# The first two pairs of the first feed-forward in two parts by feature chunks, with their loads and steps in another order

## The chip, the cores and the metric

One core of one Trainium2 chip. The metric is the time of one execution in microseconds on the device: 1695.61 us, the median of three runs (1691.41 to 1696.17).

## The reference

One layer of a decoder: a feed-forward (SwiGLU), a token mixer, a second feed-forward, each behind an RMS norm and a shift and scale that are made from a conditioning vector. What matters here is the start:

```
m = silu(c) @ w_ada + b_ada                     # 9 vectors: sh1, sc1, g1, sh2, ...
h = rms_norm(x, n1_g) * (1 + sc1) + sh1
x = x + 0.5 * g1 * (silu(h @ w1_gate) * (h @ w1_up)) @ w1_down
```

x has 512 prompt tokens and 64 sample tokens of 1024 features; the conditioning vector is one for the prompt and one for each of 8 samples. All is float32.

## The kernel before, in words

The tokens stand in the free dimension, 576 of them, in two halves of 288; the 1024 features are 8 chunks of 128 partitions. A float32 product is made of three products of rounded parts: weights and values are each split into a high part (ScalarE, a copy in the rounded type) and a low part (VectorE, the source minus the high part), and `prod` issues high x high, high x low and low x high. A column block of 128 of w1_gate together with the same block of w1_up is a pair. Pairs 0 and 1 are made by `Plain` in four product steps each, with 4 feature chunks per step: h0a (weights n11 and n21, from the first 512 rows, by the operand N11), h1a (the same weights by N1), h0b (weights a12 and a22, from rows 512 to 1023, by B21) and h1b (the same by B22). Each step is 24 products of 128x288, 12 into each of two PSUM banks. Pair 2 and those after it are made by `Pair`, in seven steps of 12, of which P1 (a11 by N11) is the first. The products of pairs 0 and 1 are 192.

The operands need the modulation. The class `First` loads the columns of sh1 and sc1 out of w_ada in four parts of 256 features each: part p covers chunks 2p and 2p+1, in 8 loads of 128x512. For each part there are these steps: mm (8 matmuls by the conditioning vectors, TensorE, L283), M (a copy out of PSUM, ScalarE, L289), tr (4 transposes, TensorE, L295), m (a sum over groups, the bias and the gain a1: three VectorE operations, L300, L304, L363). Then the chunks are normed and modulated: xr (x by the row of reciprocal norms, VectorE, L509), b0 and b1 (scale and bias of the prompt's tokens, ScalarE, L516), s (the same for the sample tokens, VectorE, L525). Operand N11 is minus the first half of chunks 0 to 3, N1 the difference of the halves there (tx is that difference), B21 and B22 are the halves of chunks 4 to 7. The number in N11h0 or B21l3 is the part, h and l are the high and low split. So N11 and N1 need parts 0 and 1, B21 and B22 parts 2 and 3. The sums T2, N3 and N4 are made in place behind them for pair 2. rw is a product with ones on TensorE (L1046) that spreads the reciprocal norms to all partitions, and rr its copy out of PSUM (L1051, L1052); every xr waits for rr.

The order is written out by hand in the table `BEGIN`: `run` executes the steps in its order and adds dependencies, so that on each engine the instructions stand in this order, whatever is ready earlier. The steps nh and nl are the splits of the first half of a pair's weights, wh and wl of the second; sn copies the result of the first half of a pair out of PSUM; xt and xc bring x into place; p2... are the splits and sums of pair 2's weights; e... are the gating, G... the split of a finished pair.

The loads go through one queue of SyncE in the order of the code from L999 to L1007: x, then parts 0 and 1, pair 0 (both halves), part 2, pair 1 (both halves), part 3, pair 2. The raw weights share four buffers (`raw4`), so that pair 2's loads wait for the low splits of earlier ones. B21 and B22 take the buffers of part 2, N3 and N4 those of part 3, so N3h and N4h wait for mm3.

Of the kernel before, what the change touches and what calls it, by code (L numbers as in the profile page):

```python
# [38 lines left out]
BEGIN = """
xt0 xt1 xc0 xt2 xc1 xt3 xc2 xt4 xc3 s5 xt5 xc4 r5 r50 r51 r52 xt6 dg xc5 xt7 xc6 rw xS xc7  # L40
rr xr0 xr3 mm0 xr2 M0 tr0 xr1 mm1 m0 nh0 s0 M1 nl0 b00 tr1 b01 m1 wh0 tx0 b10 s1 b11 wl0
N11h0 N11h1 N11l0 N1h0 N11l1 mm2 tx1 N1l0 N1h1 h0a0 T2a1 M2 N1l1 nh1 T2a0 wh1 nl1 tr2 sn0
h1a0 m2 wl1 b20 b21 s2 B21h2 T2b0 B22h2 h0a1 B21l2 T2h0 N3c0 N4c0 N3h0 T2l0 N4h0 N3l0 mm3
B22l2 sn1 N4l0 M3 tr3 h1a1 m3 b30 s3 b31 B21h3 N3c1 p2ah B21l3 T2b1 h0b1 B22h3 p2al p2bh
T2h1 N3h1 N4c1 B22l3 N4h1 p2S h0b0 T2l1 p2U p2bl p2Sh N3l1 h1b0 p2V N4l1 p2Sl e0s0 e0s1 e0m0
e0m1 h1b1 e1a0 p2Uh e1t0 e1s0 p2Ul e1m0 Gh0 P1 e1a1 e1t1 e1s1 Gl0 P2 e1m1 P1s Gh1 Gl1 P5 P6
P5s P6s
"""
# [31 lines left out]
def layer_kernel(ctx: ExitStack, tc: tile.TileContext, a):  # L80
# [390 lines left out]
    def cost(kc):  # L471
        return kc * 3 * 0.1225
# [124 lines left out]
                else:  # L597
                    st[f"b{p}{c}0"] = lambda p=p, c=c: O.b(2 * p + c, HALF[0])

    def pair_steps(p, greg):  # L600
# [20 lines left out]
        return st

    def prod(ps, w, x, fresh):
        (wh, wl), (xh, xl) = w, x
        for j in range(4):
            for z, (s, m) in enumerate(((wh, xh), (wh, xl), (wl, xh))):
                PE.matmul(  # L627
                    ps[:, :H], lhsT=s[:, j * P:(j + 1) * P], rhs=m[:, j, :],
                    start=fresh and j == 0 and z == 0, stop=j == 3 and z == 2, skip_group_check=True,
                )  # L630
# [45 lines left out]
    class Plain(Weights):  # L676


        def __init__(self, cols, n):
# [1 line left out]
            for z in range(2):
                t = raw4([2, 4, P])
                for i in range(2):
                    self.block_of(t[:, i], i, z)
                self.raw.append(t.rearrange("p m k c -> p m (k c)"))
# [1330 lines left out]
```

## Time and profile before

| | us |
|---|---|
| median of three runs | 1695.61 |
| lowest, highest | 1691.41, 1696.17 |
| the profiled execution: its time | 1692.46 |
| its span (first to last instruction) | 1690.4 |
| TensorE busy in the span | 1650.0 |
| VectorE, ScalarE busy | 1155.7, 784.2 |

The span is what the trace covers; the time of the execution holds 2.06 us more. A step's instructions are found by their lines, and two steps of the same line by their time and their tiles: xa and xs are the buffers of the parts and operands, whl and whs the split weights, wraw the raw weights, hb the normed x, ps a PSUM bank. An engine is the bound of a stretch if it has no idle time there; idle time in front of an instruction is shown with what ended it. TensorE, VectorE, ScalarE, GpSimd and SyncE are PE, DVE, ACT, POOL and SP in the rows, and PEld is the loading of weights into the array.

### The profile page before, as it was taken

The page shows a single profiled execution, that of the slowest core. Times are in us where ns is not written, and L with a number is a line of the kernel's source. Part 1 is how long each engine was busy: PE and PEld are TensorE (multiplying, and loading weights), DVE is VectorE, ACT ScalarE, POOL GpSimd, SP SyncE. Part 2 cuts the span into 40 slices and gives each one's busy share as a digit, 9 for nine tenths or more (in the row PEclk, how much of TensorE's full clock was granted, in tenths as well). Part 3 has the DMA queues.
Part 4 walks back from the last instruction along what each step waited for, and adds up shares of the span by engine and source line. Part 5 has one row for each costly group of instructions (what it writes and reads, how often), then busy time and mean ns, then how long its engine had stood idle before and what let it go on. Part 6 is the DMA issues. An engine that isn't in the chain of part 4 may idle for free.

```text
span 1690.4 us, 31360 instructions
## 1 busy us (share of the span) xinstructions
PE 1650.0 (98%) x12548; PEld 1590.6 (94%) x12548; DVE 1155.7 (68%) x1835; ACT 784.2 (46%) x1331; POOL 288.9 (17%) x372
## 2 busy tenths in 40 slices
PE   7999999999999999999999999998999999999997
PEld 4899999999999998899999999997999999999997
DVE  6867847576797776655697564676748858676773
ACT  5534524344655565544444444443236525343454
POOL 0000000000311111013245442443331000000002
PEclk9999999999999999999999999998999999999999
DMA  9443443342546766664457474898350333232331
GB/s 318 131 146 101 147 140 113 114 123 86 155 146 212 225 187 204 207 209 143 152 181 241 143 176 147 219 250 271 110 180 1 97 91 91 86 99 76 97 92 57
DMA packets 300212, 252.09 MB, mean 149 GB/s; under 512 B 13593, under 2 KB 260633, under 8 KB 300066
## 3 DMA queue, kind: packets, MB, share of 16 engines
q1 hardware_dynamic: 284594, 206.76, 40.3%
q0 software_dynamic: 13168, 40.97, 8.6%
q10 hardware_dynamic: 2304, 2.36, 0.4%
q8 instruction: 98, 1.61, 0.4%
q14 instruction: 48, 0.39, 0.1%
HBM read 207.01 MB, written 43.02 MB: 148 GB/s over the span
## 4 chain that ended last, share of the span: by engine, by line
PE 91%; DVE 3%; DMA 2%; issue 1%; ACT 1%; SPq 1%; POOL 0%; DVEq 0%; POOLq 0%; ACTq 0%
PE ps L627 45%; PE ps L461 30%; PE ps L1325 5%; PE ps L1548 2%; PE ps L283 2%; DMA xa<-in_w_ada_dram 1%; PE ps L1336 1%; PE ps L1415 1%; PE ps L1453 1%; PE ps L1459 1%; PE ps L1431 0%; PE ps L1353 0%; PE ps L295 0%; DMA c<-in_gm_ln_g_dram 0%; DMA xt<-in_x_sample_dram 0%
## 5 line engine op out<-in xcount | busy, mean ns | idle before, releaser
L627 PE MATMUL ps<-xa,whl 128*128 128x288 f32 x3000 | 428.4, 297 | 4.6 <-ACT whl L645 1.4
L627 PEld LDWEIGHTS ps<-xa,whl 128*128 128x128 f32 x3000 | 408.9, 189 | 17.6 <-issue 4.2
L627 PE MATMUL ps<-xs,whl 128*128 128x288 f32 x2040 | 294.1, 297 | 3.4 <-ACT sn L636 3.4
L627 PEld LDWEIGHTS ps<-xs,whl 128*128 128x128 f32 x2040 | 278.5, 189 | 13.5 <-ACT sn L636 6.2
L655 DVE TENSOR_TENSOR whl<-wraw,whl 128x1024 fp32r<-128x1024 f32 x192 | 234.6, 1225 | 58.0 <-ACT whl L645 50.4
L645 ACT CAST whl<-wraw 128x1024 fp32r<-128x1024 f32 x192 | 200.3, 1048 | 104.6 <-DVE wraw L769 61.2
L461 PE MATMUL ps<-c,wd 128*128 128x288 f32 x1824 | 246.1, 295 | 0.0
L461 PEld LDWEIGHTS ps<-c,wd 128*128 128x128 f32 x1824 | 242.9, 188 | 3.4 <-issue 3.4
L461 PE MATMUL ps<-c,whl 128*128 128x288 f32 x1368 | 191.6, 299 | 4.3 <-DVE S L1492 3.2
L461 PEld LDWEIGHTS ps<-c,whl 128*128 128x128 f32 x1368 | 184.6, 189 | 6.3 <-DVE S L1492 3.9
L448 POOL TENSOR_TENSOR x<-x,s 128x64 f32<-128x64 f32 x72 | 34.3, 477 | 814.8 <-DVE s L447 813.2
L442 DVE SCALAR_TENSOR_TENSOR x<-ps,gate,x 128x288 f32<-128x288 f32 (+1 forms) x128 | 61.2, 481 | 118.6 <-PE ps L461 118.5
L165 DVE TENSOR_TENSOR whl<-wraw,whl 128x1024 fp32r<-128x1024 f32 x56 | 77.9, 1393 | 75.8 <-ACT whl L164 73.1
L636 ACT COPY sn<-ps 128x288 f32<-128x288 f32 x195 | 77.4, 398 | 107.3 <-PE ps L627 106.5
L928 ACT CAST wd<-wraw 128x640 fp32r<-128x640 f32 (+2 forms) x58 | 45.3, 781 | 106.9 <-PE ps L461 101.4
L1325 PE MATMUL ps<-whl,xx 128*128 128x256 f32 x768 | 91.6, 279 | 0.0
L1325 PEld LDWEIGHTS ps<-whl,xx 128*128 128x128 f32 x768 | 90.7, 188 | 0.0
L164 ACT CAST whl<-wraw 128x1024 fp32r<-128x1024 f32 x56 | 58.6, 1048 | 31.8 <-PE ps L461 23.2
L627 PE MATMUL ps<-xs,whs 128*128 128x288 f32 x480 | 70.2, 295 | 0.0
L645 ACT CAST whs<-wraw 128x512 fp32r<-128x512 f32 x62 | 38.4, 620 | 66.8 <-PE ps L627 59.2
L627 PEld LDWEIGHTS ps<-xs,whs 128*128 128x128 f32 x480 | 65.7, 188 | 0.0
L933 DVE TENSOR_TENSOR wd<-wraw,wd 128x640 fp32r<-128x640 f32 (+2 forms) x58 | 53.9, 930 | 9.9 <-ACT wd L928 9.8
(285 smaller groups left out, 2226.7 us busy)
## 6 DMA issues: line engine op xcount, KB each, us to landing
ada<-in_w_ada_dram SPq DMA_DIRECT2D x56, 512.0 KB
wraw<-in_w_in_dram SPq DMA_DIRECT2D x96, 256.0 KB
wraw<-in_w_gate_dram SPq DMA_DIRECT2D x88, 256.0 KB
wraw<-in_w_up_dram SPq DMA_DIRECT2D x88, 256.0 KB
...
```

The costliest lines, as they stand in the source:

```text
L164: ACT.copy(out=hi, in_=raw)
L165: (eng or DVE).tensor_tensor(out=lo, in0=raw, in1=hi.bitcast(F32), op=ALU.subtract)
L442: DVE.scalar_tensor_tensor(out=x[:, o:o + w], in0=ps[:, :w], scalar=g[:, c, 0:1], in1=x[:, o:o + w], op0=ALU.mult, op1=ALU.add)
L448: return lambda: POOL.tensor_tensor(out=x[:, NP:T], in0=x[:, NP:T], in1=u, op=ALU.add)
L461: PE.matmul(ps[:, :H], lhsT=s[:, k, c0:c0 + P], rhs=m[:, HALF[h]], start=k == 0 and z == 0, stop=k == kc - 1 and z == 2,)
L627: PE.matmul(ps[:, :H], lhsT=s[:, j * P:(j + 1) * P], rhs=m[:, j, :], start=fresh and j == 0 and z == 0, stop=j == 3 and z == 2, skip_group ...
L636: ACT.copy(out=t, in_=ps[:, :H])
L645: ACT.copy(out=hl[:, 0], in_=src)
L655: DVE.tensor_tensor(out=hl[:, 1], in0=src, in1=hl[:, 0].bitcast(F32), op=ALU.subtract)
L928: ACT.copy(out=hl[:, 0], in_=self.raw[c])
L933: DVE.tensor_tensor(out=lo, in0=self.raw[c], in1=hi.bitcast(F32), op=ALU.subtract)
L1325: PE.matmul(ps[:, :DV], lhsT=s, rhs=m, start=i == 0, stop=i == 23)
```

## The change

The steps h0a, h1a, h0b and h1b of pairs 0 and 1 are cut into two each: h0a and h0c, h1a and h1c, h0b and h0d, h1b and h1d. Each is 12 products, over two feature chunks instead of four, so that a step needs one part of the modulation: a needs part 0, c part 1, b part 2, d part 3. The loads of the first two pairs are cut in halves and stand between the parts: part 0, first half of pair 0, part 1, first half of pair 1, part 2, second half of pair 0, part 3, second half of pair 1, pair 2. And `BEGIN` is written anew from mm0 on.

```
+    def part(self, name):
+        t = "AD"[int(name[1])]
+        z, js = {"a": (0, (0, 1)), "c": (0, (2, 3)), "b": (1, (0, 1)), "d": (1, (2, 3))}[name[2]]
+        if name[2] == "a":
+            setattr(self, t, [bank() for _ in range(2)])
+        x = (("N11", "B21"), ("N1", "B22"))[int(name[1])][z]
+        for ps, w in zip(getattr(self, t), (("n11", "n21"), ("a12", "a22"))[z]):
+            prod(ps, self.w[w], op(x), z == 0, js)
...
-    def prod(ps, w, x, fresh):
+    def prod(ps, w, x, fresh, js=range(4)):
...
-        for j in range(4):
+        for j in js:
...
-    parts = [First(0), First(1)]
...
-    pairs = {0: Plain(cols(w1, 0), 0)}
-    parts.append(First(2))
-    pairs[1] = Plain(cols(w1, 1), 1)
-    parts.append(First(3))
+    pairs, parts = {i: Plain(cols(w1, i), i, ()) for i in range(2)}, []
+    for p in range(4):
+        parts.append(First(p))
+        pairs[p % 2].load(p // 2)
...
-rr xr0 xr3 mm0 xr2 M0 tr0 xr1 mm1 m0 nh0 s0 M1 nl0 b00 tr1 b01 m1 wh0 tx0 b10 s1 b11 wl0
+rr xr0 m0 b00 b01 s0 mm1 M1 N11h0 nh0 N11l0 nl0 tx0 h0a0 xr1 tr1 N1h0 m1 N1l0 b10 b11 s1 nh1 h1a0
```

Three places show what this does to the order of instructions. The first is TensorE right behind the transposes of x: h by ones is rw, xa by cs is mm0, ident by ada is tr0. Before:

```order
L1046 MATMUL ps_294<-h_276,ones 128x128
L1046 MATMUL ps_294<-h_278,ones 128x128
L1046 MATMUL ps_294<-h_280,ones 128x128
L1046 MATMUL ps_294<-h_282,ones 128x128
L1046 MATMUL ps_295<-h_284,ones 128x64
L283 MATMUL ps_312<-xa_150,cs 32x512 x4
L283 MATMUL ps_312<-xa_155,cs 32x512 x4
L295 MATMUL ps_324<-ident,ada_322 128x128 x4
```

and now:

```order
L282 MATMUL ps_294<-xa_150,cs 32x512 x4
L282 MATMUL ps_294<-xa_155,cs 32x512 x4
L1061 MATMUL ps_303<-h_276,ones 128x128
L1061 MATMUL ps_303<-h_278,ones 128x128
L1061 MATMUL ps_303<-h_280,ones 128x128
L1061 MATMUL ps_303<-h_282,ones 128x128
L1061 MATMUL ps_304<-h_284,ones 128x64
L294 MATMUL ps_314<-ident,ada_310 128x128 x4
```

mm0 has moved ahead of rw. The second place is TensorE around the mm steps of parts 2 and 3: xs_28 and xs_29 are part 2, xs_32 and xa_197 (now xs_31 and xa_194) part 3, and a row with whl is one bank of a product step. Before, from mm2 to tr3:

```order
L283 MATMUL ps_377<-xs_28_176,cs 32x512 x4
L283 MATMUL ps_377<-xs_29_181,cs 32x512 x4
L627 MATMUL ps_390<-xa_370,whl_343 128x288 x12
L627 MATMUL ps_391<-xa_370,whl_343 128x288 x12
L295 MATMUL ps_426<-ident,ada_417 128x128 x4
L627 MATMUL ps_435<-xa_374,whl_343 128x288 x12
L627 MATMUL ps_436<-xa_374,whl_343 128x288 x12
L627 MATMUL ps_475<-xa_370,whl_420 128x288 x12
L627 MATMUL ps_476<-xa_370,whl_420 128x288 x12
L283 MATMUL ps_512<-xs_32_192,cs 32x512 x4
L283 MATMUL ps_512<-xa_197,cs 32x512 x4
L295 MATMUL ps_529<-ident,ada_527 128x128 x4
```

and now, from the last of the six steps on N11 and N1 (h0c1) to tr3; xs_84 is B21 and xs_85 is B22:

```order
L630 MATMUL ps_407<-xa_346,whl_385 128x288 x6
L630 MATMUL ps_408<-xa_346,whl_385 128x288 x6
L282 MATMUL ps_469<-xs_28_176,cs 32x512 x4
L282 MATMUL ps_469<-xs_29_181,cs 32x512 x4
L294 MATMUL ps_481<-ident,ada_478 128x128 x4
L630 MATMUL ps_354<-xs_84_497,whl_490 128x288 x6
L630 MATMUL ps_355<-xs_84_497,whl_490 128x288 x6
L630 MATMUL ps_387<-xs_85_501,whl_490 128x288 x6
L630 MATMUL ps_388<-xs_85_501,whl_490 128x288 x6
L282 MATMUL ps_536<-xs_31_189,cs 32x512 x4
L282 MATMUL ps_536<-xa_194,cs 32x512 x4
L294 MATMUL ps_547<-ident,ada_545 128x128 x4
```

mm2 has moved behind six of the half steps (h0a0, h1a0, h0a1, h0c0, h1c0, h0c1), and h0b0 and h1b0 stand between it and mm3. The third place is ScalarE between the copies M of parts 2 and 3 (the rows with ada); hb by mT and a is b, xs and xa are operands' high parts, whl a weight's high part, sn and the h at its side a copy sn. Before, from b of part 2 to M3:

```order
L516 ACTIVATE hb_309<-hb_309,mT,a_149 128x512 x2
L542 CAST xs_81_470<-hb_309 128x576
L542 CAST xs_82_473<-hb_309 128x576
L542 CAST xa_502<-hb_309 128x576
L542 CAST xs_86_506<-hb_309 128x576
L542 CAST xa_509<-hb_309 128x576
L636 COPY sn_522<-ps_475 128x288
L636 COPY h_524<-ps_476 128x288
L289 COPY ada_527<-ps_512 128x512
```

and now, from M2 to wh1:

```order
L288 COPY ada_478<-ps_469 128x512
L648 CAST whl_490<-wraw_186 128x1024
L515 ACTIVATE hb_325<-hb_325,mT,a_149 128x512 x2
L541 CAST xs_84_497<-hb_325 128x576
L541 CAST xs_85_501<-hb_325 128x576
L541 CAST xa_517<-hb_325 128x576
L541 CAST xs_87_521<-hb_325 128x576
L288 COPY ada_545<-ps_536 128x512
L648 CAST whl_556<-wraw_199 128x1024
```

The split of pair 0's second half (whl_490) now stands between M2 and b of part 2, and that of pair 1 (whl_556) behind M3. On VectorE the low parts wl0 and wl1 stand behind the m steps of parts 2 and 3 in the same way. From the first steps of the third pair on, TensorE's rows are those of before.

More of the change, by code (lines that the diff above doesn't have):

```diff
@@ L39 @@
 BEGIN = """
-xt0 xt1 xc0 xt2 xc1 xt3 xc2 xt4 xc3 s5 xt5 xc4 r5 r50 r51 r52 xt6 dg xc5 xt7 xc6 rw xS xc7
-rr xr0 xr3 mm0 xr2 M0 tr0 xr1 mm1 m0 nh0 s0 M1 nl0 b00 tr1 b01 m1 wh0 tx0 b10 s1 b11 wl0
[L42 to L47, printed above, removed]
+xt0 xt1 xc0 xt2 xc1 xt3 xc2 xt4 xc3 s5 xt5 xc4 r5 r50 r51 r52 xt6 dg xc5 xt7 xc6 mm0 rw M0 xS xc7 tr0
+rr xr0 m0 b00 b01 s0 mm1 M1 N11h0 nh0 N11l0 nl0 tx0 h0a0 xr1 tr1 N1h0 m1 N1l0 b10 b11 s1 nh1 h1a0
+N11h1 nl1 tx1 N11l1 N1h1 h0a1 N1l1 h0c0 xr2 sn0 h1c0 T2a0 T2a1 h0c1 sn1 mm2 M2 xr3 tr2 m2 wh0 b20 b21
+s2 wl0 B21h2 B21l2 T2b0 B22h2 B22l2 N3c0 h0b0 T2h0 T2l0 N4c0 N3h0 h1b0 N3l0 mm3 M3 tr3 m3 wh1 b30 b31
+wl1 s3 h0b1 B21h3 B21l3 h1a1 N4h0 N4l0 B22h3 h1c1 N3c1 B22l3 p2ah T2b1 h0d0 p2al T2h1 h1d0 p2bh N3h1 T2l1
+h1b1 N4c1 h0d1 e0s0 p2S N3l1 N4h1 e0s1 p2U e0m0 p2bl p2Sh h1d1 N4l1 e0m1 p2V e1a0 p2Sl p2Uh
+e1t0 e1s0 p2Ul P1 e1m0 Gh0 e1a1 e1t1 e1s1 Gl0 P2 e1m1 P1s Gh1 Gl1 P5 P6 P5s P6s
 """
@@ L598, in norm_steps, with pair_steps @@
                     st[f"b{p}{c}0"] = lambda p=p, c=c: O.b(2 * p + c, HALF[0])
-    def pair_steps(p, greg):
+    def pair_steps(p, greg, parted=False):
         st = {}
@@ L610, in pair_steps @@
         for i in range(2):
+            if parted:
+                for n in ("h0a", "h0c", "h0b", "h0d", "h1a", "h1c", "h1b", "h1d"):
+                    st[f"{n}{i}"] = lambda i=i, n=n: p[i].part(n)
             for n, f in (("nh", "nh"), ("nl", "nl"), ("wh", "wh"), ("wl", "wl"), ("h0a", "h0a"), ("sn", "snaps"),
@@ L613, in pair_steps @@
                          ("e1a", "e1a"), ("e1s", "e1s"), ("e1t", "e1t"), ("e1m", "e1m")):
-                st[f"{n}{i}"] = lambda i=i, f=f: getattr(p[i], f)()
+                st.setdefault(f"{n}{i}", lambda i=i, f=f: getattr(p[i], f)())
             st[f"Gh{i}"] = lambda i=i: G(i, lambda i: p[i].finish_hi())
@@ L630, in prod @@
                 )
-        tick(cost(4))
+        tick(cost(len(js)))
     def snap(ps, t=None):
@@ L676, in layer_kernel, with __init__, load @@
     class Plain(Weights):
-        def __init__(self, cols, n):
+        def __init__(self, cols, n, halves=range(2)):
             self.cols, self.n, self.g, self.w, self.hl, self.raw = cols, n, None, {}, {}, []
[L681 to L685, printed above, removed]
+            for z in halves:
+                self.load(z)
+        def load(self, z):
+            t = raw4([2, 4, P])
+            for i in range(2):
+                self.block_of(t[:, i], i, z)
+            self.raw.append(t.rearrange("p m k c -> p m (k c)"))
+        def part(self, name):
[6 more added lines that the diff above has]
+                prod(ps, self.w[w], op(x), z == 0, js)
         def nh(self):
@@ L1066, in layer_kernel @@
     ops["near"] = ("B21", "B22", "N3")
-    steps = {**operand_steps(Late()), **pair_steps(pairs, greg)}
+    steps = {**operand_steps(Late()), **pair_steps(pairs, greg, True)}
     for c in range(KC):
```

## The prediction

> **What bounds the kernel now.** I read the page first, then the busy times by stretch, then the timeline of each engine up to 70 us. The page says that TensorE is the bound, and the stretches say where:
>
> ```profile
> span 1690.4 us, 31360 instructions
> PE 1650.0 (98%) x12548; PEld 1590.6 (94%) x12548; DVE 1155.7 (68%) x1835; ACT 784.2 (46%) x1331; POOL 288.9 (17%) x372
> ```
>
> In the stretches the columns are length, busy time and count of PE, PEld, DVE, ACT and POOL, then the granted clock, the share of the DMA engines and GB/s:
>
> ```profile
> 0.00:5.00 5.00, 0.68 (x7) 0.71 (x8) 0.00 (x0) 2.34 (x2) 1.40 (x11) 1.00 0.49 140
> 5.00:10.00 5.00, 2.84 (x11) 1.64 (x11) 0.93 (x2) 1.87 (x5) 0.00 (x0) 1.00 1.01 302
> 10.00:15.00 5.00, 5.00 (x20) 3.21 (x19) 2.24 (x5) 4.95 (x17) 0.00 (x0) 1.00 1.09 328
> 15.00:20.00 5.00, 5.00 (x20) 3.66 (x21) 4.12 (x13) 1.33 (x2) 0.00 (x0) 1.00 1.09 384
> 45.00:50.00 5.00, 3.04 (x28) 1.84 (x21) 3.72 (x9) 2.60 (x6) 0.00 (x0) 0.95 0.78 247
> 50.00:55.00 5.00, 5.00 (x29) 5.00 (x29) 4.03 (x7) 4.97 (x8) 0.00 (x0) 0.71 0.36 105
> 48.35:100.00 51.65, 51.65 (x375) 49.54 (x376) 42.19 (x69) 29.29 (x47) 0.00 (x0) 0.97 0.38 113
> 100.00:200.00 100.00, 100.00 (x752) 95.98 (x751) 69.46 (x116) 41.20 (x66) 3.60 (x8) 1.00 0.44 130
> 200.00:400.00 200.00, 199.98 (x1501) 193.59 (x1500) 138.06 (x225) 81.59 (x129) 6.58 (x16) 1.00 0.41 118
> ```
>
> From 48.35 to 400 us TensorE has no gap worth naming (199.98 of 200.00 in the last row). So a change that touches only the first 70 us is worth what it does to one moment: the start of P1, the first product step of the third pair, behind which the two kernels queue the same products. A shift of P1 passes through to the end about one to one.
>
> The PE timeline up to P1 (columns: start, length, engine, line, operation, count, in brackets the idle time before it and what ended it). L1046 is rw, L283 an mm step, L295 a tr step, L627 products:
>
> ```profile
> 18.86 2.69 PE L1046 MATMUL ps<-h,ones 128*128 128x128 f32 x10
> 21.48 3.64 PE L283 MATMUL ps<-xa,cs 128*32 128x512 f32 x16
> 25.90 0.66 PE L295 MATMUL ps<-ident,ada 128*128 128x128 f32 x4 [0.78 <-ACT ada L289]
> 26.49 1.92 PE L283 MATMUL ps<-xa,cs 128*32 128x512 f32 x16
> 29.25 0.66 PE L295 MATMUL ps<-ident,ada 128*128 128x128 f32 x4 [0.84 <-ACT ada L289]
> 32.22 1.69 PE L283 MATMUL ps<-xs,cs 128*32 128x512 f32 x4 [0.26 <-DMA xs<-in_w_ada_dram]
> 33.84 3.87 PE L627 MATMUL ps<-xa,whl 128*128 128x288 f32 x24
> 37.91 6.63 PE L627 MATMUL ps<-xa,whl 128*128 128x288 f32 x48
> 44.47 1.07 PE L283 MATMUL ps<-xs,cs 128*32 128x512 f32 x8
> 45.35 1.04 PE L283 MATMUL ps<-xa,cs 128*32 128x512 f32 x8
> 48.35 0.66 PE L295 MATMUL ps<-ident,ada 128*128 128x128 f32 x4 [1.96 <-ACT ada L289]
> 48.76 4.95 PE L627 MATMUL ps<-xa,whl 128*128 128x288 f32 x24
> 53.55 12.96 PE L627 MATMUL ps<-xs,whl 128*128 128x288 f32 x96
> 66.34 1.76 PE L627 MATMUL ps<-xa,whl 128*128 128x288 f32 x12
> ```
>
> To be seen here: all four mm steps are behind TensorE by 46.4 us, with 72 of the 192 products of pairs 0 and 1 put between them; mm2 ran as soon as its weights came (32.22, a DMA ended the wait). From 48.35 on, 120 products stand back to back until P1 at **66.34**. One product costs 12.79 / 96 = 0.133 us at full clock (53.55 to 66.34). The 24 at 48.76 took 4.79 instead of 3.2, in the stretch whose clock is 0.71: the gap behind mm3 cost **1.6 us** of clock besides its own length.
>
> **The change, part by part.** The work is the same: the 192 products, the four mm and tr steps, the splits, the bytes. Sixteen more rows in PE's order are only groups of 12 cut into 6 and 6. So P1 moves by what PE waits, and that follows from the order. Two effects are free. The loads: the same 14.0 MB (x, c and vec 2.45, four parts of 2.1, three pairs of 1.05, by the tile shapes) come in another order, and nothing below waits for them; part 0 is there when mm0 can start, since 4.55 MB stand ahead of its end in the queue, and the first four rows above bring 0.70, 1.51 and 1.64 by 15 us and the rest by about 17. The buffers of pair 3's second load come free only after wl1 (about 61 us, before: by 44), but its products stand 11 us behind P1. If I am wrong on that cover, it costs the few us of one load.
>
> What costs is the path from the x turns to P1. Its lengths are these rows, of ACT (rowr is rr, L289 is M, L643 is nh, L516 is b, L540 and L542 are the high parts) and of DVE (L509 is xr, four of them; L300 to L363 is m; L651 is nl; L559 is tx; L551 a low part):
>
> ```profile
> 20.97 0.58 ACT L1051 COPY rowr<-ps 128x512 f32<-128x512 f32 x1 [4.62 <-PE ps L1046]
> 25.74 1.06 ACT L643 ACTIVATE whl<-wraw 128x1024 fp32r<-128x1024 f32 x1
> 28.61 0.58 ACT L289 COPY ada<-ps 128x512 f32<-128x512 f32 x1 [1.81 <-PE ps L283]
> 29.09 1.52 ACT L516 ACTIVATE hb<-hb,mT,a 128x512 f32<-128x512 f32 x2
> 32.87 1.24 ACT L540 ACTIVATE xa<-hb 128x576 fp32r<-128x576 f32 x2
> 41.73 1.25 ACT L542 CAST xs<-hb 128x576 fp32r<-128x576 f32 x2
> 21.83 5.17 DVE L509 TENSOR_TENSOR hb<-x,rowr 128x1152 f32<-128x1152 f32 x4 [1.43 <-ACT rowr L1052]
> 26.91 0.30 DVE L300 TENSOR_REDUCE m<-ps 128x36 f32<-128x144 f32 x1
> 27.48 0.18 DVE L363 SCALAR_TENSOR_TENSOR a<-mT,vec 128x18 f32<-128x18 f32 x1
> 28.22 1.22 DVE L651 SCALAR_TENSOR_TENSOR whl<-wraw,whl 128x1024 fp32r<-128x1024 f32 x1
> 29.94 0.31 DVE L300 TENSOR_REDUCE m<-ps 128x36 f32<-128x144 f32 x1 [0.50 <-PE ps L295]
> 30.64 0.76 DVE L559 TENSOR_TENSOR tx<-hb 128x576 f32<-128x576 f32 x1
> 43.02 0.75 DVE L551 TENSOR_TENSOR xs<-hb,xs 128x576 fp32r<-128x576 f32 x1
> ```
>
> An m step is 26.91 to 27.66, so 0.75. From the start of an mm step to the start of its m step, through M and tr, is 26.49 to 29.94: 3.45. A half product step is 12 x 0.133 = 1.6; when it waits for a low part, 10 of its 12 products come after that: 1.35.
>
> *Up to the first half step.* mm0 and rw swap places: together 18.86 to 25.1 as before, but rr, 2.1 behind the start of rw, now waits for mm0 (3.64): it ends at about 25.4 instead of 21.8. Then, in the written order, xr0 (5.17 / 4 = 1.3) 26.7, m0 27.5, b00 and b01 29.0, M1 29.5, N11h0 30.2, nh0 31.2 on ACT, nl0 32.4 on DVE, and the ten products of h0a0 33.8. tr0 and mm1 were done at about 27.5, so PE waits 3.7 us here.
>
> *Up to mm2.* tr1 stands behind h0a0 on PE although M1 was ready at 29.5: tr1 34.5, m1 35.2, b10 and b11 36.8, nh1 37.8, N11h1 38.4; on DVE nl1 39.1, tx1 39.8, N11l1 40.5. So h0c0 ends at 41.9, and h1c0 and h0c1 at **45.1**. Only then comes mm2, whose data landed by about 33, since all six half steps stand ahead of it.
>
> *Up to mm3.* m2 starts 3.45 behind, 48.6, ends 49.4; b20 and b21 51.0, B21h2 51.7, B21l2 52.4, h0b0 53.8, h1b0 55.4. mm3 stands behind these.
>
> *Up to P1.* m3 starts at 58.8 and ends at 59.6; wl1, behind it on DVE, 60.8; h0b1 62.2. h1a1 and h1c1, which need nothing from parts 2 and 3, are queued behind h0b1 and wait with it. From there no operand is late: the seven half steps h1a1, h1c1, h0d0, h1d0, h1b1, h0d1, h1d1 take 11.2. **P1 at 73.4** at full clock, 7.1 later.
>
> As a check from the other side: from the end of mm1 to P1 PE has 192 x 0.133 = 25.5, two mm (3.8) and three tr (1.5), 30.9 us of work, in both kernels. Before, 28.41 to 66.34 leaves 7.0 for waits and the low clock; now 27.5 to 73.4 leaves 15.0.
>
> *The clock.* An mm matmul took 1061 ns at 21.5 us and 592 at 26.5:
>
> ```profile
> L283 PE MATMUL ps<-xa,cs x16: 1059/1061/1062, 21.5 to 24.1; 128*32 128x512 f32 x16
> L283 PE MATMUL ps<-xa,cs x16: 592/592/617, 26.5 to 27.8; 128*32 128x512 f32 x16
> ```
>
> so mm0 at 18.86 is costed at 3.64 (if it ran at 1.92, all is 1.7 earlier). Before, one gap of 1.96 us and a tr cost 1.6 us. Now there are three gaps: 27.5 to 31.2; 47.0 to 51.7 with only a tr in it; 57.3 to about 60.8, with a tr and two products. Behind the first, only 1.35 us of h0a0 stand on the path. Bounds: none costs anything (0), or each costs 1.6 (4.8). I take the two later ones, 3.2, since PE runs on the path right behind them. P1 at 76.6: **10.3 us later**. The Trainium skill (TensorE: Matmul & The Clock Gate, section HAM oscillation) has a rule against this change: gaps of more than about 3.4 us put the array back on half clock, and work behind each starts cold. By it the first two gaps count surely, and the third about evenly; the sum would be 7.1 and 1.35 + 1.6 to 3.2, 10 to 12. The trace is stricter than the rule: a gap of 1.96 us was enough at 49.5.
>
> Sum: the profiled execution took 1692.46 (span 1690.4 and 2.06 around it); 1692.46 + 10.3 = 1702.8. The runs shown had 1691.41, 1695.61 and 1696.17, a median 3.15 above the profiled one, which would give 1705.9. I forecast **1704**.
>
> How this can be read in the order of instructions: in TensorE's rows shown above with the change, no product stands ahead of mm2 in the kernel before, and those between mm2 and mm3 need parts 0 and 1 alone, which are there. Now 72 products stand ahead of mm2, and those between tr2 and mm3 need B21 and B22, the operands that are made out of mm2's own result, through ACT's b and high parts and DVE's low parts. That is why PE runs dry twice, behind mm2 and behind mm3.
>
> **The rivals.** *It does what it says: products fill the waits.* PE would have only its 30.9 us from 27.5 to P1, so P1 at 58.4, 7.9 earlier: 1692.46 - 7.9 = 1684.6. For it: the loads and PE's share allow it. Against it: h0a0 cannot start before nh0, and mm2, h0b0 and mm3 form a chain in which each waits for ACT and DVE work on the part before. It decides on PE's waits from mm1 to P1: under 2.8 us the kernel is faster by over 0.3%, which is 5.1 us and about what a measurement of this kernel can tell from no change. I have 15.0. Chance 0.04.
>
> *The vector work is quicker than its sum.* If mm0 runs at full clock (1.7 earlier) and no gap costs clock, the shift is 7.1 - 1.7 = 5.4; a further 1 us less of waits makes it no difference: 1697 to 1701. Chance 0.14.
>
> *Every gap costs its clock*, and the half clock in h0a0 moves tr1 too: 7.1 + 4.8 = 11.9, and up to 14 if a gap spans two spells of half clock: 1704.4 to 1709. Chance 0.25. The forecast's own case has the rest, 0.57.
>
> **How the numbers follow.** The forecast, the quick case's upper part and most of the third case give 8 in 10: from 1692.46 + 5.0 = 1697.5 to 1695.6 + 13.4 = 1709. Slower by over 0.3%: 0.57 + 0.25 = 0.82; within 0.3%: 0.14; faster: 0.04.
>
> **What would show it.** Right: in the PE timeline of the changed kernel mm2 starts at 43 to 47 and mm3 at 53 to 59, both with data long landed; PE idles about 15 us between mm1 and P1, ended by ACT and DVE; P1 stands at 73 to 79; the granted clock falls below 1 in two or three stretches before 70 us; from P1 on the timeline is that of before, shifted. Wrong: mm2 before 38 us, or h0a0 before 29, or P1 at or before 66; or a shift at P1 that is gone at 400 us.

## The result, and the profile after

The changed kernel took **1704.43 us** (median of 4 runs, 1702.73 to 1705.58) against 1695.38 for the kernel before (4 runs, 1691.41 to 1696.17): a ratio of 1.0063, 95% interval 1.0048 to 1.0078. By the medians it is slower by 9.05 us. The ratio is an estimate over the runs and not the quotient of the two medians (1.0053): by it the difference is 10.7 us, with 8.1 to 13.2 in the interval. Its profiled execution took 1704.38 us.

The page of the profile: TensorE is the bound as before, with the same number of matmuls.

```profile
span 1702.4 us, 31365 instructions
PE 1655.1 (97%) x12548; PEld 1594.8 (94%) x12548; DVE 1154.9 (68%) x1835; ACT 785.6 (46%) x1331; POOL 289.0 (17%) x372
```

PE's timeline of the changed kernel up to P1 (L282 is an mm step, L1061 rw, L294 tr, L630 products):

```profile
18.43 2.64 PE L282 MATMUL ps<-xa,cs 128*32 128x512 f32 x16
21.00 1.52 PE L1061 MATMUL ps<-h,ones 128*128 128x128 f32 x10
...
23.04 3.45 PE L282 MATMUL ps<-xa,cs 128*32 128x512 f32 x16
28.74 0.53 PE L630 MATMUL ps<-xa,whl 128*128 128x288 f32 x2 [2.26 <-ACT whl L646]
30.00 2.64 PE L630 MATMUL ps<-xa,whl 128*128 128x288 f32 x10 [0.72 <-DVE whl L654]
...
44.43 1.92 PE L282 MATMUL ps<-xs,cs 128*32 128x512 f32 x16
47.13 0.66 PE L294 MATMUL ps<-ident,ada 128*128 128x128 f32 x4 [0.79 <-ACT ada L288]
50.89 0.61 PE L630 MATMUL ps<-xs,whl 128*128 128x288 f32 x1 [3.10 <-ACT xs L541]
51.68 5.89 PE L630 MATMUL ps<-xs,whl 128*128 128x288 f32 x23 [0.18 <-DVE xs L550]
57.50 1.06 PE L282 MATMUL ps<-xs,cs 128*32 128x512 f32 x8
...
62.86 1.59 PE L630 MATMUL ps<-xs,whl 128*128 128x288 f32 x10 [1.18 <-DVE whl L658]
...
67.49 8.16 PE L630 MATMUL ps<-xs,whl 128*128 128x288 f32 x60
75.49 1.76 PE L630 MATMUL ps<-xa,whl 128*128 128x288 f32 x12
```

mm2 starts at 44.43 and mm3 at 57.50, where they stood at about 30 and 44.47. Each wait printed in these rows is ended by ScalarE or VectorE, none by a load (one wait for a load hides inside the row of mm1; see old_loads). P1 starts at 75.49, 9.15 us later than before; the medians differ by 9.05. The stretches of the changed kernel (columns as in the prediction: the granted clock is the third number from the end):

```profile
30.00:32.00 2.00, 2.00 (x9) 2.00 (x10) 1.88 (x2) 0.68 (x1) 0.00 (x0) 0.54 1.11 366
32.00:34.00 2.00, 1.73 (x8) 1.41 (x7) 0.43 (x2) 0.00 (x0) 0.00 (x0) 0.60 1.12 370
...
50.00:52.00 2.00, 0.93 (x2) 0.61 (x3) 1.50 (x3) 1.38 (x3) 0.00 (x0) 0.66 0.09 23
52.00:54.00 2.00, 2.00 (x9) 2.00 (x9) 2.00 (x4) 0.67 (x1) 0.00 (x0) 0.50 1.01 272
54.00:56.00 2.00, 2.00 (x10) 2.00 (x10) 0.97 (x2) 0.00 (x0) 0.00 (x0) 0.50 0.66 238
56.00:58.00 2.00, 2.00 (x15) 1.43 (x18) 0.00 (x0) 0.00 (x0) 0.00 (x0) 0.63 0.00 0
...
200.00:400.00 200.00, 199.92 (x1501) 193.58 (x1500) 136.75 (x226) 81.43 (x128) 6.57 (x16) 1.00 0.41 120
```

The clock is at half behind the first pause (30 to 34) and for most of 51 to 57.5 behind the second, where 23 products took 5.89 us instead of 23 x 0.133 = 3.1; behind the third it is full. From P1 on there is nothing new: 199.92 of 200 us are busy.

### The profile page after: what moved, and what is told of

Read it like the earlier page. It is cut to its first block, busy times and chain, and to the rows that moved or that the text cites. A ratio compares the mean times of both kernels' runs of the same rounds, so it can differ in the third digit from the quotient of the medians.

```text
span 1702.4 us, 31365 instructions
## 1 busy us (share of the span) xinstructions
PE 1655.1 (97%) x12548; PEld 1594.8 (94%) x12548; DVE 1154.9 (68%) x1835; ACT 785.6 (46%) x1331; POOL 289.0 (17%) x372
## 4 chain that ended last, share of the span: by engine, by line
PE 85%; issue 5%; DVE 3%; DMA 3%; ACT 2%; POOL 1%; SPq 1%; POOLq 0%; DVEq 0%; ACTq 0%
PE ps L630 40%; PE ps L460 30%; PE ps L1340 5%; PE ps L1563 2%; PE ps L282 1%; PE ps L1351 1%; PE ps L1430 1%; PE ps L1468 1%; DMA xa<-in_w_ada_dram 1%; DMA wraw<-in_w_in_dram 1%; DVE whl L658 1%; PE ps L1474 1%; PE ps L1446 0%; PE ps L1368 0%; PE ps L294 0%
## 5 line engine op out<-in xcount | busy, mean ns | idle before, releaser
L630 PE MATMUL ps<-xa,whl 128*128 128x288 f32 x3000 | 430.3, 298 | 9.6 <-ACT whl L646 2.3
L630 PEld LDWEIGHTS ps<-xa,whl 128*128 128x128 f32 x3000 | 410.1, 190 | 23.4 <-issue 5.0
L630 PE MATMUL ps<-xs,whl 128*128 128x288 f32 x2040 | 297.8, 299 | 7.7 <-ACT xs L541 3.1
L630 PEld LDWEIGHTS ps<-xs,whl 128*128 128x128 f32 x2040 | 281.2, 190 | 18.8 <-ACT sn L639 5.9
L630 PE MATMUL ps<-xs,whs 128*128 128x288 f32 x480 | 70.1, 294 | 0.0
L630 PEld LDWEIGHTS ps<-xs,whs 128*128 128x128 f32 x480 | 65.7, 188 | 0.0
```

What stands on the lines that cost most here:

```text
L630: PE.matmul(ps[:, :H], lhsT=s[:, j * P:(j + 1) * P], rhs=m[:, j, :], start=fresh and j == 0 and z == 0, stop=j == 3 and z == 2, skip_group ...
```

## The experiments

My theory: PE waits longer between mm1 and P1, because mm2 and mm3 stand late and each is followed by its own turn, sums and splits with nothing to do beside them; pauses also let the clock fall; what P1 loses arrives at the end. The main rivals: the loads' order or the cut into half steps costs, or the clock is only a symptom. P1 stood at 66.34, 65.02 and 65.26 us in the three executions that have the order of before (before, half_steps, before_fill), 65.5 on average. Differences in time are of medians, each against the runs of the kernel before that were made beside it.

**old_loads**: only the loads go back to the order of before.

```diff
-    pairs, parts = {i: Plain(cols(w1, i), i, ()) for i in range(2)}, []
-    for p in range(4):
-        parts.append(First(p))
-        pairs[p % 2].load(p // 2)
+    parts = [First(0), First(1)]
+    pairs = {0: Plain(cols(w1, 0), 0)}
+    parts.append(First(2))
+    pairs[1] = Plain(cols(w1, 1), 1)
+    parts.append(First(3))
```

> The order of the steps of the changed kernel, with the order of the loads of the kernel before. Theory (the steps' order makes TensorE wait, the loads land in time either way): the first product step of pair 2 (P1) starts at 75.5 us give or take 1.5, as in the changed kernel, and the ratio to before is 1.0063 give or take 0.001. Rival (the loads' order costs the time): P1 goes back towards the 66.3 us of before, with a ratio of 1.003 or less.

Measured: 1705.30 against 1693.25 us, ratio 1.0075 (1.0061 to 1.0088). PE's timeline:

```profile
18.73 3.64 PE L282 MATMUL ps<-xa,cs 128*32 128x512 f32 x16
...
30.16 0.85 PE L630 MATMUL ps<-xa,whl 128*128 128x288 f32 x2 [3.60 <-ACT whl L646]
...
36.57 9.65 PE L630 MATMUL ps<-xa,whl 128*128 128x288 f32 x59 [1.29 <-DVE xa L550]
...
77.69 1.76 PE L630 MATMUL ps<-xa,whl 128*128 128x288 f32 x12
```

P1 is not earlier but 2.2 us later, beyond my bounds by 0.7, and the waits have the same enders. mm0 took 3.64 us here, against 2.64, so everything hung on rr came later: 1.4 us of the 2.2 stand already at h0a0 (30.16 against 28.74). The rest is the clock, which fell at other places: the 59 products from 36.57 took 9.65 instead of 59 x 0.133 = 7.9, the 23 behind the second pause 4.84 (5.89 in the changed kernel), the ten behind the third 2.48 (1.59) and the 24 behind those 4.02 (3.36). That is TensorE's speed, not a load. The new order of the loads does make mm1 wait: the changed kernel's mm1 took 3.45 us, 1.4 of them waits of its weight loads for part 1, against 1.92 here. But the copy M1 stands on ScalarE behind b0, which ended at 26.50, when that mm1 had just ended (26.49), and so nearly all of it is hidden: M1 follows the start of b0 by 1.60 us there and by 1.42 here. The rival falls.

**half_steps**: the kernel before, each step as two half steps in a row.

```diff
-N11h0 N11h1 N11l0 N1h0 N11l1 mm2 tx1 N1l0 N1h1 h0a0 T2a1 M2 N1l1 nh1 T2a0 wh1 nl1 tr2 sn0
+N11h0 N11h1 N11l0 N1h0 N11l1 mm2 tx1 N1l0 N1h1 h0a0 h0c0 T2a1 M2 N1l1 nh1 T2a0 wh1 nl1 tr2 sn0
```

> The kernel before with the eight steps of the first two pairs cut into half steps that run right behind one another; loads and order as before. Theory (cutting is free, placing costs): P1 at 66.3 us give or take 0.5, ratio 1.000 give or take 0.0007. Rival (the cut itself costs, since TensorE goes 16 times instead of 8 from one bank to the other): 9 us over 8 more changes would be 1.1 us each, and the ratio 1.005.

Measured: 1693.00 against 1693.25 us, ratio 0.9999 (0.9989 to 1.0008). PE's timeline from h0a on, with the 1.95 us pause behind mm3:

```profile
34.45 3.45 PE L631 MATMUL ps<-xa,whl 128*128 128x288 f32 x24
...
48.54 0.66 PE L295 MATMUL ps<-ident,ada 128*128 128x128 f32 x4 [1.95 <-ACT ada L289]
48.95 3.43 PE L631 MATMUL ps<-xa,whl 128*128 128x288 f32 x24
...
65.02 1.76 PE L631 MATMUL ps<-xa,whl 128*128 128x288 f32 x12
```

The cut is free. P1 is 1.3 us earlier than in the profile of before, 0.8 below my bounds, mainly because behind the same pause the 24 products took 3.43 us, not 4.95. (The first 24 took 3.45 instead of 3.87 too, but started 0.6 later, behind mm2's load.) So the 1.6 us that I priced a pause at belonged to one execution and not to the pause.

**earlier23**: the changed kernel with mm2 and mm3 (and what hangs on them) pulled ahead. Pieces of the table:

```diff
-N11h1 nl1 tx1 N11l1 N1h1 h0a1 N1l1 h0c0 xr2 sn0 h1c0 T2a0 T2a1 h0c1 sn1 mm2 M2 xr3 tr2 m2 wh0 b20 b21
+N11h1 nl1 tx1 xr2 N11l1 N1h1 mm2 h0a1 N1l1 M2 tr2 h0c0 sn0 h1c0 m2 T2a0 T2a1 h0c1 sn1 xr3 wh0 b20 b21
-s2 wl0 B21h2 B21l2 T2b0 B22h2 B22l2 N3c0 h0b0 T2h0 T2l0 N4c0 N3h0 h1b0 N3l0 mm3 M3 tr3 m3 wh1 b30 b31
+s2 wl0 B21h2 B21l2 T2b0 B22h2 B22l2 N3c0 mm3 h0b0 M3 tr3 T2h0 m3 T2l0 N4c0 h1b0 N3h0 wh1 b30 b31
```

> The changed kernel with mm2, its copy, turn and sum, and mm3 with its own, moved ahead by one or two half steps, so that products stand between mm2 and tr2, tr2 and h0b0, mm3 and tr3; loads and half steps as in the changed kernel. Theory (what costs is that each part of the modulation stands with its turn and its sum in one row on TensorE with nothing between): two pauses shrink, P1 at 71.5 us give or take 1.5, ratio 1.0038 give or take 0.001. Rival (the later start of the modulation's parts costs little, the half steps or the loads cost): P1 at 74.5 us or later, ratio 1.0055 or more.

Measured: 1699.91 against 1693.25 us, ratio 1.0039 (1.0026 to 1.0052). PE's timeline:

```profile
37.69 1.92 PE L283 MATMUL ps<-xs,cs 128*32 128x512 f32 x16
...
50.17 0.40 PE L631 MATMUL ps<-xs,whl 128*128 128x288 f32 x1 [1.70 <-ACT xs L542]
...
71.19 1.76 PE L631 MATMUL ps<-xa,whl 128*128 128x288 f32 x12
```

mm2 stands 6.7 us earlier, the wait at h0b0 is 1.70 instead of 3.10, P1 is at 71.19. As the theory had it: where the modulation's parts stand is what costs.

**split_first**: nh0 and nl0 of pair 0 ahead of the first modulated blocks.

```diff
-rr xr0 m0 b00 b01 s0 mm1 M1 N11h0 nh0 N11l0 nl0 tx0 h0a0 xr1 tr1 N1h0 m1 N1l0 b10 b11 s1 nh1 h1a0
+rr xr0 m0 nh0 b00 b01 nl0 s0 mm1 M1 N11h0 N11l0 tx0 h0a0 xr1 tr1 N1h0 m1 N1l0 b10 b11 s1 nh1 h1a0
```

> The changed kernel with the split of pair 0's first weights (nh0 on ScalarE, nl0 on VectorE) moved ahead of the first modulated blocks, into time in which ScalarE waits 2.09 us. Theory (the first pause is the queue of ScalarE and VectorE ahead of h0a0, and a wait shortened there passes on): h0a0 starts 0.7 to 1 us earlier and its second wait goes, P1 74.0 us give or take 1.2, ratio 1.0055 give or take 0.0012. Rival (the later links, m1 and what hangs on it, set the end, so nothing comes through): h0a0 earlier, but h0b0 and P1 as in the changed kernel, 75.5 us or later.

Measured: 1701.39 against 1693.59 us, ratio 1.0051 (1.0037 to 1.0066). PE's timeline:

```profile
18.18 3.64 PE L283 MATMUL ps<-xa,cs 128*32 128x512 f32 x16
...
28.52 0.40 PE L631 MATMUL ps<-xa,whl 128*128 128x288 f32 x1 [1.60 <-ACT xa L540]
29.31 1.73 PE L631 MATMUL ps<-xa,whl 128*128 128x288 f32 x11 [0.39 <-DVE xa L547]
...
73.81 1.76 PE L631 MATMUL ps<-xa,whl 128*128 128x288 f32 x12
```

Although mm0 ended 0.75 us later than in the changed kernel (18.18 + 3.64 against 18.43 + 2.64), h0a0's later products start 0.7 earlier, mm2 2.0 (42.42) and P1 1.7 earlier. The first wait is ScalarE's and VectorE's queue, and what is saved there passes on; but that is only the 0.7, and most of what comes on top up to mm2 is the clock, which stayed full behind the first pause (11 products in 1.73 us, against ten in 2.64). Two details were not as expected: h0a0's first product is only 0.2 earlier (28.52), and its second wait is shorter (0.39 instead of 0.72) and not gone.

**after_again**: the changed kernel itself, once more.

> The changed kernel once more, unchanged. Theory (where the clock falls behind a pause, and for how long, differs from one execution to the next of the same instructions): the waits behind the same engines as before within 0.5 us, but P1 not at 75.5 us, somewhere from 74 to 78, with other stretches at half clock. Rival (the clock falls at fixed places): P1 within 0.3 us of 75.49 and half clock in the same stretches. Both: ratio 1.0063 give or take 0.0015.

Measured: 1704.13 against 1693.59 us, ratio 1.0070 (1.0056 to 1.0085). PE's timeline:

```profile
18.25 3.29 PE L282 MATMUL ps<-xa,cs 128*32 128x512 f32 x16
...
51.54 4.85 PE L630 MATMUL ps<-xs,whl 128*128 128x288 f32 x23 [0.40 <-DVE xs L550]
...
61.68 2.51 PE L630 MATMUL ps<-xs,whl 128*128 128x288 f32 x10 [1.18 <-DVE whl L658]
...
75.82 1.76 PE L630 MATMUL ps<-xa,whl 128*128 128x288 f32 x12
```

and two of its stretches:

```profile
62.00:64.00 2.00, 2.00 (x11) 2.00 (x10) 1.39 (x3) 1.97 (x5) 0.00 (x0) 0.50 0.70 236
64.00:66.00 2.00, 2.00 (x12) 2.00 (x12) 2.00 (x4) 0.82 (x1) 0.00 (x0) 0.64 0.54 159
```

P1 is 0.33 us off its first place, hardly beyond the rival's bound, but made up otherwise: the 23 products behind the second pause took 4.85 and not 5.89, and the ten behind the third 2.51 and not 1.59. So the places of half clock differ between two executions of the same instructions.

The stretches also tell how long a spell of half clock lasts, since a stretch of 2 us with a clock of 0.64 was at half for 2 x 2 x 0.36 = 1.44 us, if the clock is either full or half (the undivided stretches read 1.00 or 0.50). Such a spell takes 3.44 us (62.00 to 65.44) in the rows above, and 3.44 (30.16 to 33.60) and 6.84 (50.64 to 57.48) in those of the changed kernel. The other spells before P1 have the same measure: 6.84 (31.28 to 38.12) and 3.44 (51.76 to 55.20) in after_again, 3.44 (49.52 to 52.96) in the profile of before, 10.24 in old_loads. All are one, two or three times 3.4, and between the spells of one execution lie whole multiples of it: 17.04 us from 33.60 to 50.64, 13.64 from 38.12 to 51.76, 6.80 from 55.20 to 62.00. So the clock changes only at points of a fixed grid of 3.4 us within an execution, wherever the pauses lie on it. A spell costs half its length, 1.7 us, where products stand back to back in it, and less where TensorE waits anyway.

**fill_both**: 16 products behind mm1 and 24 behind tr2 that nobody reads. (The second group writes to free columns of the bank in which pair 0's sum stands open, and alters that sum.)

```diff
+        for i in range(16):
+            PE.matmul(ps[:, 0:P], lhsT=ones, rhs=ident, start=True, stop=True, skip_group_check=True)
...
+        for i in range(24):
+            PE.matmul(pairs[0].A[0][:, H:512], lhsT=pairs[1].w["n11"][0][:, 0:P], rhs=op("N1")[0][:, 0, 0:512 - H], start=True, stop=True, skip_group_check=True)
```

> The changed kernel with products that nobody reads in two of TensorE's pauses: 16 of 128x128 behind mm1 and 24 of 128x224 behind tr2. The waits' causes stay as they are. Theory (part of the 9.15 us is half clock behind the pauses, about 1.3 us at h0a0 and 3 us at h0b0 and behind): the granted clock stays full from 23 to 60 us, P1 starts at 71.5 us give or take 1, ratio 1.0035 give or take 0.001. Rival (the waits alone set the time and work beside them is hidden): P1 at 74.5 us or later, ratio 1.0055 or more.

Measured: P1 at 71.60 us, as the theory had it, but 1701.65 against 1693.25 us, ratio 1.0051 (1.0035 to 1.0066), between the two expectations.

**fill_three**: the same in a bank of their own, and a third group behind tr3.

```diff
+    steps["fill1"], steps["fill2"], steps["fill3"] = (lambda n=n, w=w: fill(n, w) for n, w in ((16, 0), (20, 1), (8, 1)))
...
-rr xr0 m0 b00 b01 s0 mm1 M1 N11h0 nh0 N11l0 nl0 tx0 h0a0 xr1 tr1 N1h0 m1 N1l0 b10 b11 s1 nh1 h1a0
+rr xr0 m0 b00 b01 s0 mm1 fill1 M1 N11h0 nh0 N11l0 nl0 tx0 h0a0 xr1 tr1 N1h0 m1 N1l0 b10 b11 s1 nh1 h1a0
```

> The changed kernel with products that nobody reads, into a bank of their own, in three pauses: 16 of 128x128 behind mm1, 20 of 128x288 behind tr2, 8 of 128x288 behind tr3. Theory (the changed kernel loses some 4 us to half clock behind its pauses, in whichever of them it falls): no half clock from 24 to 66 us, P1 at 71.6 us give or take 0.7, ratio 1.004 give or take 0.0012. Rival (the first filled kernel's other executions were slower than its profiled one, so filling gives back less): P1 at 73 us or later, or P1 at 71.6 us and a ratio of 1.0055 or more, so that the time doesn't follow P1.

Measured: 1701.19 against 1692.15 us, ratio 1.0055 (1.0043 to 1.0068). PE's timeline (L1109 and L1107 are the products that nobody reads):

```profile
26.22 3.84 PE L1109 MATMUL ps<-ident,ones 128*128 128x128 f32 x32
29.81 1.83 PE L631 MATMUL ps<-xa,whl 128*128 128x288 f32 x12
...
46.12 2.88 PE L1107 MATMUL ps<-xa,whl 128*128 128x288 f32 x20
...
50.27 3.33 PE L631 MATMUL ps<-xs,whl 128*128 128x288 f32 x23 [0.40 <-DVE xs L551]
...
71.53 1.76 PE L631 MATMUL ps<-xa,whl 128*128 128x288 f32 x12
```

The granted clock is 1.00 in every stretch from 18 to 68 us, the 23 products take 3.33, and P1 comes 4.0 us earlier than in the changed kernel (4.3 against after_again). That shows what half clock is worth up to P1. At the end less of it is seen: 9.04 us from before, against 9.05 and 10.54. By the ratios (1.0055 against 1.0063 and 1.0070) the gain is 1.4 to 2.5 us, and the intervals leave room for none of the 4.0 us as for all. The rival's last case, that the time doesn't follow P1, is just reached (1.0055), but not shown: the interval goes down to 1.0043, which my theory allows.

**gap3**: the kernel before in half steps, and one of them moved: h0b0's first half between mm3 and tr3 (with the splits that it needs, and M3, moved ahead).

```diff
-h1a0 m2 wl1 b20 b21 s2 B21h2 T2b0 B22h2 h0a1 B21l2 T2h0 N3c0 N4c0 N3h0 T2l0 N4h0 N3l0 mm3
-B22l2 sn1 N4l0 M3 tr3 h1a1 m3 b30 s3 b31 B21h3 N3c1 p2ah B21l3 T2b1 h0b1 B22h3 p2al p2bh
+h1a0 h1c0 m2 wl1 b20 b21 s2 B21h2 T2b0 B22h2 h0a1 h0c1 B21l2 T2h0 N3c0 N4c0 B22l2 T2l0 mm3 N3h0 M3 N3l0 N4h0
+sn1 N4l0 h0b0 tr3 h1a1 h1c1 m3 b30 s3 b31 B21h3 N3c1 p2ah B21l3 T2b1 h0b1 B22h3 p2al p2bh
```

> The loads and the order of the kernel before, all steps in half steps, and of these one thing moved: h0b0's first half stands between mm3 and tr3 (with B22's split ahead of N3c, N4c's), and mm3's copy ahead of sn1, so that TensorE has 12 products to do while ScalarE copies mm3's block. Theory (half steps help where they stand between a product of the modulation and its turn): the 1.95 us pause before tr3 goes, P1 at 63.4 us give or take 0.7, ratio 0.9985 give or take 0.0008. Rival (that pause is hidden or given back at the operands' splits): P1 at 64.8 us or later, ratio 0.9995 or more.

Measured: 1690.44 against 1693.59 us, ratio 0.9983 (0.9973 to 0.9993): **faster than both kernels**. PE's timeline at h0a and behind mm3:

```profile
33.68 3.46 PE L631 MATMUL ps<-xa,whl 128*128 128x288 f32 x24
...
45.76 1.87 PE L631 MATMUL ps<-xs,whl 128*128 128x288 f32 x12
47.46 0.60 PE L295 MATMUL ps<-ident,ada 128*128 128x128 f32 x4
...
62.28 1.76 PE L631 MATMUL ps<-xa,whl 128*128 128x288 f32 x12
```

The pause of 1.95 us is gone: tr3 follows the twelve products without a wait. From the start of h0a to P1 it is 28.6 us here, against 30.6 in half_steps (34.45 to 65.02): 2.0 less, the length of the pause. The other 0.8 us by which P1 is earlier come from before h0a.

**gap3_again**: the same kernel once more.

> gap3 once more, unchanged, on the chip of this call. Theory (the half step between mm3 and tr3 is worth what P1 shows): P1 at 62.3 to 63.4 us, ratio 0.998 give or take 0.001. Rival (its first measurement was a lucky one): ratio 0.9995 or more.

Measured: 1690.95 against 1694.54 us, ratio 0.9987 (0.9978 to 0.9997), P1 at 63.61. PE's timeline:

```profile
35.02 3.46 PE L631 MATMUL ps<-xa,whl 128*128 128x288 f32 x24
...
63.61 1.76 PE L631 MATMUL ps<-xa,whl 128*128 128x288 f32 x12
```

It holds. P1 is 0.2 above my bounds and 1.3 later than in gap3, but all of that lies ahead of h0a: from there to P1 it is 28.6 us again. In the order of before mm2 waits for its load (4.5 us of waits of its weight loads here, 3.7 in gap3), and when that lands differs from execution to execution.

**gap34**: as gap3, and h0a0's first half ahead of mm2 (with N11's first split and the four xr in another order).

```diff
-rr xr0 xr3 mm0 xr2 M0 tr0 xr1 mm1 m0 nh0 s0 M1 nl0 b00 tr1 b01 m1 wh0 tx0 b10 s1 b11 wl0
-N11h0 N11h1 N11l0 N1h0 N11l1 mm2 tx1 N1l0 N1h1 h0a0 T2a1 M2 N1l1 nh1 T2a0 wh1 nl1 tr2 sn0
+rr xr0 mm0 xr1 M0 tr0 mm1 m0 nh0 s0 M1 nl0 b00 tr1 b01 m1 N11h0 tx0 N11l0 b10 s1 b11 h0a0 mm2 xr2 xr3
+N1h0 N11h1 N11l1 wh0 tx1 N1l0 N1h1 h0c0 T2a1 M2 N1l1 nh1 T2a0 wl0 nl1 tr2 sn0
```

> As gap3, and pair 0's first half step of h0a also stands ahead of mm2 (with N11's first split ahead of the weights' and x's third and fourth products behind it on VectorE), where TensorE waits 1.05 us for mm2's load. Theory (the same): P1 at 62.5 us give or take 0.8, ratio 0.998 give or take 0.0008. Rival (h0a0 can't start before its splits, so TensorE waits for ScalarE or VectorE there as in the changed kernel and nothing is won over gap3): P1 at 63.4 us or later, ratio 0.9985 or more.

Measured: 1689.95 against 1693.59 us, ratio 0.9983 (0.9973 to 0.9993). PE's timeline:

```profile
30.98 0.40 PE L631 MATMUL ps<-xa,whl 128*128 128x288 f32 x1 [1.48 <-ACT xa L540]
31.77 3.01 PE L631 MATMUL ps<-xa,whl 128*128 128x288 f32 x11 [0.39 <-DVE xa L547]
...
63.77 1.76 PE L631 MATMUL ps<-xa,whl 128*128 128x288 f32 x12
```

The rival's case, as far as P1 shows (63.77, beyond the 63.3 of my bounds): h0a0 waits 1.48 us for ScalarE there, as in the changed kernel, the clock falls (11 products in 3.01 us), and nothing shows over gap3.

**gap34_fill**: as gap34, with 6 products that nobody reads behind tr1.

```diff
+        for i in range(6):
+            PE.matmul(ps[:, 0:P], lhsT=ones, rhs=ident, start=True, stop=True)
```

> As gap34, with 6 products of 128x128 that nobody reads behind tr1, in the 1.48 us in which TensorE waits for the first half step of h0a0. Theory (that pause let the clock fall to half for 12 products and a part of mm2): full clock throughout from 24 us, P1 at 62.3 us give or take 0.8, ratio 0.9975 give or take 0.0008. Rival (mm2 waits for its load there anyway, so the faster half step only waits longer): P1 at 63.4 us or later, ratio 0.9983 or more.

Measured: P1 at 62.56 us, the 11 products in 1.73, as the theory had it; but 1691.82 against 1692.15 us, ratio 0.9996 (0.9987 to 1.0005), which the theory had not.

**before_fill**: the same 6 products in the kernel before, between tr1 and mm2.

> The kernel before with 6 products of 128x128 that nobody reads between tr1 and mm2, where TensorE waits for mm2's load anyway. All three filled kernels measured 2.5 to 3.3 us more than their P1 gives one to one (8.4, 9.0 and -0.3 us from before, against 5.9, 5.9 and -3.1). Theory A (such products cost nothing by themselves; the differences are dips of the clock later in the run, which fall otherwise in each execution): P1 65 to 66.4 us, ratio 1.000 give or take 0.0008. Theory B (filling costs something later in the run whatever it does at its place): P1 the same, ratio 1.0015 or more.

Measured: P1 at 65.26 us, 1693.94 against 1694.54 us, ratio 1.0002 (0.9993 to 1.0010). Such products cost nothing by themselves, at that place. All together (rest is the profiled span less P1, difference that of the medians):

| | P1, us | P1 less 65.5 | difference, us | rest, us |
|---|---|---|---|---|
| before | 66.34 | | | 1624.1 |
| half_steps | 65.02 | -0.5 | -0.25 | 1625.3 |
| before_fill | 65.26 | -0.2 | -0.60 | 1625.2 |
| changed | 75.49 | 10.0 | 9.05 | 1626.9 |
| after_again | 75.82 | 10.3 | 10.54 | 1624.5 |
| old_loads | 77.69 | 12.2 | 12.05 | 1628.0 |
| earlier23 | 71.19 | 5.7 | 6.66 | 1627.6 |
| split_first | 73.81 | 8.3 | 7.80 | 1627.3 |
| gap3 | 62.28 | -3.2 | -3.15 | 1621.1 |
| gap3_again | 63.61 | -1.9 | -3.59 | 1627.7 |
| gap34 | 63.77 | -1.7 | -3.64 | 1625.7 |
| fill_both | 71.60 | 6.1 | 8.40 | 1622.9 |
| fill_three | 71.53 | 6.0 | 9.04 | 1627.7 |
| gap34_fill | 62.56 | -2.9 | -0.33 | 1627.4 |

Without filling, time follows P1 within 2 us. With it, three of four kernels are 2.3 to 3.0 us slower than their P1. For two of them the interval of the ratio excludes what P1 would give (fill_three: 7.3 to 11.5 us against 6.0; gap34_fill: -2.2 to 0.8 against -2.9), for fill_both it does not (5.9 to 11.2 against 6.1); and each P1 is that of one execution. The rest from P1 to the end holds the same work in all, and lies between 1621.1 and 1628.0 in single executions: 2.4 apart for the changed kernel and after_again, 6.6 for gap3 and gap3_again. Half clock makes a part of that: the mean granted clock over the span is 0.996 in gap3's profile and 0.992 in gap3_again's, which is some 13 and 27 us at half. A place where it arises, in the changed kernel:

```profile
460.00:464.00 4.00, 4.00 (x21) 4.00 (x20) 1.13 (x2) 3.38 (x7) 0.93 (x2) 0.57 0.21 74
```

and in after_again, with the same instructions and ten products more in the same time:

```profile
460.00:464.00 4.00, 4.00 (x31) 3.90 (x30) 1.12 (x3) 3.27 (x7) 1.21 (x2) 1.00 0.21 74
```

Why the time, over several executions, should be longer than P1 gives for kernels whose start is filled is not settled. More half clock later on does not show as the cause: the mean clock of fill_three's five executions is 0.9926, 25 us at half, none of them up to P1 in the profiled one; that of the changed kernel's four is 0.9888, 38 us, of which 10 lie up to P1 in the profiled one. Behind P1 the two are about alike.

## Why the prediction was right, step by step

The forecast was 1704.0 us for a measured 1704.43. The mechanism is the one it named; the closeness is in part luck, because two terms were off in opposite directions, the start and the waits 1.9 us too long together and the clock 0.8 too small, and because 1704 was a choice between the 1702.8 and 1705.9 that the two bases gave. The shift says it better: 10.3 us forecast, 9.15 and 9.5 at P1 in two executions, 9.05 and 10.54 in the medians.

- *P1 passes to the end one to one.* Right within the noise: 9.15 us at P1, 9.05 in the medians and 10.7 by the ratio, and within 2 us in all kernels without filling. A single execution is blurred by what falls behind P1, though: the profiled execution ends 12.0 us behind the one of before (1702.4 less 1690.4), and the 2.9 beyond P1's shift do not stand in the medians.
- *The loads and the cut are free.* Right: old_loads and half_steps. That nothing waits for the loads was not quite so: mm1 did, and ScalarE's queue hid it.
- *The path.* The times of its marks:

| us | forecast | changed | after_again | fill_three |
|---|---|---|---|---|
| rest of h0a0 starts | 32.4 | 30.00 | 30.28 | 29.81 (all 12) |
| mm2 starts | 45.1 | 44.43 | 44.29 | 43.00 |
| rest of h0b0 starts | 52.4 | 51.68 | 51.54 | 50.27 |
| mm3 starts | 55.4 | 57.50 | 56.32 | 53.53 |
| last ten of h0b1 start | 60.8 | 62.86 | 61.68 | 58.90 |
| P1, full clock | 73.4 | | | 71.53 |
| P1 | 76.6 | 75.49 | 75.82 | |

- *The start was mis-sized.* I costed mm0 at 3.64, since the 16 matmuls took that before, and rw with it at its old 2.69. In the profile after, the block began 0.4 earlier and the array was at full speed sooner, 2.64 and 1.52, so the block ended at 22.5 and not at 25.1, and everything hung on rr came earlier. (The granted clock reads 1.00 in the changed kernel's stretches before 30 us; that the array is at half speed there at first is read from the lengths alone, 1061 and 592 ns for the same matmul.) It is not the same each time: mm0 took 2.64, 3.29, 3.64, 3.02, 3.64, 2.69 and 2.98 us in the seven executions that have it first (the changed kernel, after_again, old_loads, earlier23, split_first, fill_both, fill_three).
- *The waits were right.* From the end of mm1 to P1 at full clock, fill_three has 71.53 - 26.29 = 45.2 us, of which 30.9 are work: 14.3 of waits, for a forecast of 15.0. (The idle time that the trace itself shows from mm1 to P1 is less, 11.4 us in the changed kernel: its busy time also holds gaps between products inside a row.) Before, by half_steps, 26.09 + 1.92 = 28.0 to 65.02 leaves 6.1.
- *The clock was mis-sized.* I took 3.2 us from the two later pauses and none from the first. Measured by fill_three it is 75.49 - 71.53 = 4.0 in the changed kernel and 4.3 in after_again. By the table, the changed kernel lost 1.4 of it between h0a0 and mm2 (44.43 against 43.00), 2.6 between h0b0 and mm3, where the spell of 6.84 us lies, and nothing behind the third pause. after_again lost 1.3, 1.5 and 1.5, with half clock behind each pause, the last over the ten products (2.51) and the 24 behind them (4.00 instead of 3.36). So the first pause does count, and my price of 1.6 is that of one spell of 3.4 us, not of a pause. The Trainium skill (TensorE: Matmul & The Clock Gate, section What's actually happening) says why that can differ: the window of about 3.4 us by which the clock is granted runs freely, so that its phase decides. The traces agree: half clock lasts one, two or three times 3.4 us, on one grid within an execution, and the same instructions lost clock at other places in another. Why a pause brings one spell, two or none is not shown here.
- *The rivals.* "Products fill the waits" came nowhere near: mm1 to P1 had 14.3 us of waits where it allowed 2.8. The point of "the vector work is quicker" without clock cost, 5.4 us at P1, is what fill_three reached at P1 (71.53, against 66.34 + 5.4 = 71.7), so what kept the changed kernel from it is the clock. "Every gap costs its clock" is half right: two of three did in the changed kernel's profile, all three in after_again; but there they cost 4.3 together and not 4.8, and with the earlier start P1 came 9.5 us later, not 11.9.
- *The signs.* mm2, mm3 and P1 lay inside their bounds; the waits were 14.3 us beside the work and 11.4 as idle time, for "about 15". One sign of "wrong" showed: h0a0 before 29. Its first two products started at 28.74, the others at 30.00. I had set that mark by a start that was more than a microsecond late.
